# A two-branch encoder layer: the first request group's head by channel quarters, branch B's inverse rms through DRAM, the gate's adaLN in column strips

## The chip, the cores and the metric

The kernel runs on one core of a Trainium2 chip. The metric is the device time of one execution in microseconds (us), taken as the median of several runs. TensorE, VectorE, ScalarE and GpSimd compute, each with its own stream of instructions; all DMAs are issued from SyncE's queue.

## What is computed

The same layer, with the same weights, is applied to two request groups (prompt and sample), each 1024 tokens of 1024 channels, all in float32.

```python
mod = silu(c) @ w_ada + b_ada
shift, scale, gate = split(mod, 3)
h = rms_norm(x, norm_g) * (1 + scale) + shift
qa, ka, va, za, qb, kb, vb, zb, ga, gb = split(h @ w_in)
# branch A: 8 query heads, 2 key/value heads of 64; QK rms norm, axial rotary
oa = attention(qa, ka, va) * silu(za)
# branch B: 4 heads, two softmax maps each, values of 128
ob = softmax(q1 k1) v - lam * softmax(q2 k2) v
ob = rms_norm(ob, subln_g) * (1 - lam_init) * silu(zb)
merged = sigmoid(ga) * (oa @ w_proj_a) + sigmoid(gb) * (ob @ w_proj_b)
y = x + gate * (merged @ w_out)
```

## The kernel before

Every large product is made in three matmuls: each operand is held as a rounded high part and a low part (`split_w`, L175: ScalarE rounds, VectorE subtracts), and high x high, high x low and low x high are added up in PSUM. `x` is held with channels on the partitions: eight chunks of 128 channels, two halves of 512 tokens (`ht[hf]`, the normalised rows, as high and low parts). One bank of a gate product (`z_gen`, L693: za, zb, ga, gb) is 24 matmuls of 512 columns at L704; there are 48 banks in each group, in 12 items of four. One tile of 128 tokens of a q, k or v product (`proj_tt`, L506) is 24 matmuls of 256 columns at L515.

**The head of the first group** (`start`, L337). adaLN's shift and scale are made from eight loads of 1 MB of `w_ada` (`load_ada`, L243), each with four float32 matmuls of 512 columns whose stationary operand is `cT`, two columns (`ada`, L292, L298). `ada_end` (L300) copies the two rows, turns them into columns with four small matmuls (L307) and adds the bias (L311, L315). The first 512 tokens' squares (L254) are added up on VectorE (`added`, L257) and summed over the partitions by matmuls with a column of ones (`inv_rms`, L266, L271); GpSimd takes the power, `spread` (L281) makes of it a tile over all partitions. `modulated` (L317) scales, shifts and splits. The second 512 tokens' squares aren't added first, so L271 runs eight times as often for them; `start_late` (L368) modulates them. Projections come behind all adaLN matmuls. The key/value weights are loaded early into `p` tiles; the other weights pass through three `st` tiles.

**Order.** The kernel writes its pieces of work as generators, and `weave` (L71) sets their order: of several streams, each with a nominal number of steps and an offset, the one with the least progress is next. A scheduler then orders each engine's instructions with that order as priority, by a model of time, and can pull later work forward where buffers allow. `head` (L1020) weaves the key/value products (`kva_gen`), the first half of branch A's queries (`qa_gen`) and gate banks (`Z_HEAD`, in banks). Then `phase` (L1115) weaves six stages of attention: two of branch A's 16 units and four of branch B's four, each with the next products and with `Z_SHARE` gate banks. In the last stage `fill` (L1142) runs beside the attention: for the first group the gate's adaLN (`gate_gen`, L445; 16 loads, 16 float32 matmuls at L452), the gate banks that are left, and the first `16 - TAIL` merge pieces of branch A (`merge_gen`, L954; 12 matmuls of 512 columns at L976 each). `TAIL` merge pieces stand behind the attention, then branch B's merge, then the output product (L1007) with the second group's normalisation beside it.

**An attention unit** has scores (L737, L738), a maximum on VectorE (L739), the exponential on ScalarE (L741), for branch B a difference of two maps (L773), a block transpose on VectorE (L774) with four DMAs that put the blocks in place (`flip`, L767, L779), and the values (L799, L800 or L839). Branch B's squares are summed by matmuls at L861; GpSimd takes the inverse rms (L869) once a head's four units are through.

**Gating** (`gated_gen`, L912) reads attention output and gate back from DRAM, multiplies them with the row factor, and splits. Branch A's row factors (inverse softmax sums) are transposed once, written to a DRAM row `rA` (L921), and read back spread over the partitions into `tab` tiles (L936; two buffers, which also hold the rotary tables). Branch B's are transposed by TensorE into a PSUM bank, four transposes for each half of each head (L942); VectorE multiplies from there (L943, L947).

Tiles come from pools: 15 `u` tiles of 1 MB, two `w` tiles for split weights, four `p`, three `st` and three `row` tiles, one `ev` tile; in PSUM two `s` tiles of two banks (scores), three `f` banks and one `a` bank. `gbank` (L120) also hands out score banks while no attention runs.

## Time and profile before

| | |
|---|---|
| median of 3 runs | 1940.68 us (1940.3 to 1945.74) |
| the profiled execution | 1933.24 us |
| its span, first to last instruction | 1931.5 us |
| mean granted TensorE clock | 0.995 |
| first exponential of the first group's attention | 141.5 us |
| last matmul at L452 (gate's adaLN) | 767.8 us |
| last power of branch B's inverse rms, first group | 849.4 us |

The lines below are from the profiled execution. A row of the timeline gives start, duration, engine, line, operation and tiles (`f<-u,cT` is: writes `f`, reads `u` and `cT`), the count of instructions merged in it, and in brackets how long the engine stood idle before it and what it waited for. A row of the chain of waits gives start, duration, and the engine, tile and line on the chain. A row of a group gives busy time, mean duration in ns, idle time before. A row by stretches gives the stretch, its length, busy time with number of instructions on each engine (TensorE, its weight loads, VectorE, ScalarE, GpSimd), the granted clock, the DMA engines' share and GB/s. A float32 matmul shows as two rows.

### The profile page before, as it was taken

To read this page: it belongs to the slowest core of one execution; us is meant where nothing else is said; L and a number is where in the kernel's file an instruction comes from. 1 tells how busy PE (TensorE), PEld (TensorE's weight loads), DVE (VectorE), ACT (ScalarE), POOL (GpSimd) and SP (SyncE) were. 2 spreads that over 40 slices of the span, in tenths; PEclk is the share of its full clock that TensorE was granted. 3 is DMA by queue.
4 is the path that set the end of the run, shared out by engine and by line. 5 is a ranking of instruction groups with operands and counts; after the bars stand their busy time and mean duration, and the time that the engine had idled before them with its cause. 6 is when DMAs were issued, how large, how long until landed. Compare 5 with 4: busy or idle time off the path is not lost.

```text
span 1931.5 us, 30797 instructions
## 1 busy us (share of the span) xinstructions
PE 1881.2 (97%) x10466; PEld 1610.0 (83%) x10466; DVE 1397.3 (72%) x2145; ACT 991.7 (51%) x2091; POOL 414.7 (21%) x758
## 2 busy tenths in 40 slices
PE   8899999999999999999999999999989999999999
PEld 3788888888988995778889888898877989888887
DVE  5669886778898677767465788688788767777731
ACT  4446665666666454414233566566666545542310
POOL 1342300120335051000124231013221524201000
PEclk9999999999999999999999999999999999999999
DMA  9125465556554436875641455565545343477522
GB/s 319 45 81 146 135 173 148 153 148 176 152 142 110 116 92 192 273 256 181 218 140 39 137 144 166 145 172 151 154 129 162 107 113 100 143 234 264 180 104 77
DMA packets 271613, 295.25 MB, mean 153 GB/s; under 512 B 37857, under 2 KB 220257, under 8 KB 271457
## 3 DMA queue, kind: packets, MB, share of 16 engines
q1 hardware_dynamic: 271456, 293.28, 51.4%
q8 instruction: 84, 1.38, 0.3%
q14 instruction: 73, 0.59, 0.1%
HBM read 133.72 MB, written 42.01 MB: 91 GB/s over the span
## 4 chain that ended last, share of the span: by engine, by line
PE 81%; DVE 7%; DMA 5%; issue 2%; ACT 2%; SPq 1%; POOL 1%; DVEq 0%; ACTq 0%; POOLq 0%
PE f L704 22%; PE f L515 19%; PE f L1007 5%; PE s L737 5%; PE a L839 5%; PE s L738 5%; PE f L976 4%; PE s L1007 4%; PE a L800 3%; PE a L799 3%; PE s L976 2%; DMA q<-p 2%; DVE m L739 2%; DVE p L774 1%; PE f L298 1%
## 5 line engine op out<-in xcount | busy, mean ns | idle before, releaser
L704 PE MATMUL f<-u,w 128*128 128x512 f32 x2232 | 574.2, 395 | 2.0 <-DVE ssB L863 1.5
L515 PE MATMUL f<-w,u 128*128 128x256 f32 x3456 | 487.5, 285 | 7.5 <-DVE u L571 3.7
L515 PEld LDWEIGHTS f<-w,u 128*128 128x128 f32 x3456 | 457.8, 190 | 29.0 <-DVE u L571 4.3
L704 PEld LDWEIGHTS f<-u,w 128*128 128x128 f32 x2232 | 404.2, 188 | 77.8 <-DVE ssB L863 1.8
L739 DVE TENSOR_REDUCE m<-s 128x1 f32<-128x1024 f32 x256 | 311.0, 1217 | 51.3 <-PE s L738 48.4
L774 DVE STREAM_TRANSPOSE p<-p 128x1024 f32<-128x1024 f32 x192 | 238.3, 1241 | 92.7 <-ACT p L741 89.3
L738 PE MATMUL s<-u,sw 128*128 128x512 f32 x512 | 203.8, 398 | 0.0
L788 DVE TENSOR_TENSOR q<-q,hi 128x512 fp32r<-128x512 f32 x256 | 171.5, 690 | 34.3 <-ACT hi L787 32.3
L787 ACT ACTIVATE hi<-q 128x512 fp32r<-128x512 f32 x256 | 153.6, 624 | 76.2 <-DMA q<-p 37.8
L741 ACT ACTIVATE p<-s,m,rsA 128x1024 f32<-128x1024 f32 x128 | 153.8, 1202 | 71.4 <-DMA q<-p 69.6
L178 ACT ACTIVATE w<-st 128x512 fp32r<-128x512 f32 x196 | 114.4, 625 | 99.2 <-DMA st<-in_w_in_dram 42.4
L741 ACT ACTIVATE p<-s,m,rsB 128x1024 f32<-128x1024 f32 x128 | 154.3, 1205 | 6.5 <-DMA q<-p 1.9
L179 DVE TENSOR_TENSOR w<-st,w 128x512 fp32r<-128x512 f32 x196 | 132.8, 706 | 34.2 <-ACT w L178 33.1
L658 POOL TENSOR_TENSOR row<-row,gB 128x96 f32<-128x96 f32 x64 | 33.8, 528 | 485.7 <-ACT row L529 474.1
L799 PE MATMUL a<-hi,u 128*128 128x256 f32 x512 | 132.2, 284 | 2.8 <-DMA q<-p 1.8
L800 PE MATMUL a<-q,u 128*128 128x256 f32 x512 | 129.3, 286 | 2.6 <-DVE q L788 2.6
L976 PE MATMUL f<-u,w 128*128 128x512 f32 x540 | 130.5, 393 | 1.3 <-DVE u L987 1.3
L839 PE MATMUL a<-q,u 128*128 128x256 f32 x512 | 127.1, 385 | 3.9 <-DVE oo L816 3.0
L976 PEld LDWEIGHTS f<-u,w 128*128 128x128 f32 x540 | 100.5, 188 | 23.0 <-DVE u L987 2.3
L839 PEld LDWEIGHTS a<-q,u 128*128 128x128 f32 x512 | 95.6, 193 | 20.0 <-DVE oo L816 3.6
L737 PE MATMUL s<-u 128*128 128x512 f32 x256 | 108.3, 424 | 3.3 <-ACT p L741 3.2
L737 PE MATMUL s<-u,u 128*128 128x512 f32 x256 | 102.4, 400 | 8.5 <-ACT p L741 3.1
(181 smaller groups left out, 2557.5 us busy)
## 6 DMA issues: line engine op xcount, KB each, us to landing
q<-p SPq DMA_DIRECT2D x768, 128.0 KB, 2.6
st<-in_w_in_dram SPq DMA_DIRECT2D x132, 256.0 KB, 3.1
zd<-ev SPq DMA_DIRECT2D x96, 256.0 KB, 2.2
sw<-u SPq DMA_DIRECT2D x256, 64.0 KB, 2.1
p<-zd SPq DMA_DIRECT2D x64, 256.0 KB, 3.7
u<-in_w_ada_dram SPq DMA_DIRECT2D x8, 1024.0 KB, 10.4
st<-in_w_in_dram SPq DMA_DIRECT2D x64, 128.0 KB, 2.8
st<-in_w_out_dram SPq DMA_DIRECT2D x32, 256.0 KB, 3.6
```

The lines of the kernel that those rows point to most:

```text
L515: nc.tensor.matmul(ps, lt[c][:, sl], w[:, c, wi, :], start=(k == 0), stop=(k == 23))
L704: nc.tensor.matmul(ps, w[:, c, wi, e * P : (e + 1) * P], rt[c], start=(k == 0), stop=(k == 23),)
L737: nc.tensor.matmul(s[:, sl], q, k[:, sl], start=True, stop=False)
L738: nc.tensor.matmul(s[:, sl], sw, k[:, sl], start=False, stop=True)
L739: nc.vector.tensor_reduce(out=m, in_=s, axis=AX.X, op=ALU.max, negate=True)
L741: nc.scalar.activation(pt.rearrange("p (j c a) -> p j c a", j=4, c=8), s.rearrange("p (c a j) -> p j c a", c=8, j=4), AF.Exp, scale=rs, bi ...
L774: nc.vector.transpose(pt, pt)
L799: nc.tensor.matmul(acc, lt, th[:, c, :], start=(k == 0), stop=False)
L800: nc.tensor.matmul(acc, lt, tl[:, c, :], start=False, stop=(k == 7))
L839: nc.tensor.matmul(acc, u["v"][:, k], pT[:, k], start=(k == 0), stop=(k == 7))
L976: nc.tensor.matmul(ps, w[:, c, wi, d * P : (d + 1) * P], o[:, oi, :], start=(k == 0), stop=(k == 11))
L1007: nc.tensor.matmul(ps, w[:, c, wi, e * P : (e + 1) * P], m[:, mi, :], start=(k == 0), stop=(k == 23))
```

## The change

- **The first group's head goes by channel quarters.** `xT` is loaded first; an adaLN load now holds shift and scale of 256 channels, so two loads give a quarter. Its matmuls go to four column strips of the array (`tile_position`), one for each input chunk, with `cT` padded to 32 columns; the strips' sums are added by four small matmuls with a two-column selector (`ada_sum`). For each quarter: multiply by the inverse rms, modulate, the key/value and za products of its two channel chunks (`kva_early`, `z_one`, into four and two PSUM regions held open), then the next quarter's adaLN. za's first weights are loaded early too, za's second go into `u` tiles. These instructions keep their program order on their engines (`in_order`).
- **The late rows** (second 512 tokens): squares added up on VectorE first; their inverse rms and modulation are split into two calls; modulated in two halves. za's four banks for them are made chunk by chunk (`z_first`).
- **The gate's adaLN** moves to the head, woven with `qa`, in loads of 256 by 256 and matmuls of 256 columns in four column strips.
- **Branch B's inverse rms**: 16 rows (two heads) are transposed at once, copied, written to DRAM (`rB`) and read back spread into a `tab` tile, as branch A's.
- **Numbers**: shares, weights and offsets of `weave`, now per group where they weren't.

```diff
-    (7, 19, 6, 3, 2, 4),
-    (9, 14, 7, 3, 2, 6),
+    (8, 23, 6, 1, 1, 2),
+    (13, 12, 7, 3, 0, 6),
 )
-Z_HEAD = (6, 5)
+Z_HEAD = (9, 6)
...
-LAST_ATT = 44
-LAST_FILL = 26
-GATED_A = -0.3
-TAIL = 5
-TAIL_A = 0.3
+LAST_ATT = (45, 45)
+LAST_FILL = (20, 25)
+GATED_A = (0.12, 0.1)
+GATE_A = 0.0
+TAIL = (2, 3)
+TAIL_A = (1.15, 1.15)
+Z_FIRST = (22, 7)
+Z_FIRST_A = (-0.05, -0.1)
...
+        total, *rest = [q[:, i : i + 2] for q in sq for i in (0, 2)]
+        for x in rest:
+            nc.vector.tensor_tensor(out=total, in0=total, in1=x, op=ALU.add)
+        nc.vector.tensor_tensor(out=total[:, 0], in0=total[:, 0], in1=total[:, 1], op=ALU.add)
...
+    def ada(wts, cpad):
+
+        acc = gbank()
+        for q, wt in enumerate(wts):
+            for c in range(4):
+                pe.matmul(
+                    acc[32 * c : 32 * c + 32], cpad[:, q * 4 + c], wt[:, c], start=(q == 0), stop=(q == 1),
+                    tile_position=(0, 32 * c),
+                )
+        part = rtile()
+        act.activation(part, acc, AF.Copy)
+        return part
...
     def modulated(ht, hf, xT, cs):
         for c in cs:
             scale, shift = modc[:, 1, c, 0:1], modc[:, 0, c, 0:1]
+            hh, hl = (x[c] for x in ht[hf][:2])
+            act.activation(hh, xT[c], AF.Identity, scale=scale, bias=shift)
+            vec.tensor_scalar(
+                out=xT[c], in0=xT[c], scalar1=scale, scalar2=shift, op0=ALU.mult, op1=ALU.add
+            )
+            vec.tensor_tensor(out=hl, in0=xT[c], in1=hh.bitcast(F32), op=ALU.subtract)
...
+        rs = inv_rms(added(squares(xT[0])))
+        rsb = spread(rs)
+        early.update(kva=[x for b in two_banks() for x in (b[:, :256], b[:, 256:])], z=two_banks())
+        ps = ada_sum(ada(wts[:2], cpad))
+        for quarter in range(4):
+            cs = range(quarter * 2, quarter * 2 + 2)
+            by_rms(xT[0], cs, rsb)
+            split_early(kva_w[0][1], quarter)
+            ada_end(quarter, ps)
+            if quarter % 2 == 0:
+                add_h(ht, 0, quarter // 2)
+            split_early(kva_w[1][1], quarter, act)
+            modulated(ht, 0, xT[0], cs)
+            split_early(kva_w[1][1], quarter, vec)
+            for c in cs:
+                kva_early(ht, c)
+            part = ada(wts[quarter * 2 + 2 : quarter * 2 + 4], cpad) if quarter < 3 else None
+            for c in cs:
+                for e in range(2):
+                    z_one(ht, 0, c, kva_w[1][0], e, early["z"][e], pe)
+                if part is not None:
+                    ps, part = ada_sum(part), None
+        xT.append(load_xT0(1))
+        kva_w.append((load_w(w_cols(w_in, (C_ZA + 256, 256)), room=(utile(), utile())),))
+        return lambda: inv_rms(added(squares(xT[1]))), lambda rs: start_late(ht, xT[1], rs)
...
+                for c in (2, 3, 0, 1):
+                    nc.tensor.matmul(
+                        acc[32 * c : 32 * c + 2], cT[:, q * 4 + c], sts[c // 2][:, c % 2], start=(q == 0), stop=(q == 1),
+                        tile_position=(0, 32 * c),
+                    )
...
+        banks = [two_banks(), two_banks()]
+        for c in range(NCH):
+            for w, bs in zip(ws, banks):
+                for e, ps in enumerate(bs):
+                    z_one(ht, 1, c, w, e, ps)
+            yield 1
...
+        if i > 1 and hf == 0:
+            ss = st["ssB"][:, 2 * i - 4 : 2 * i - 2].rearrange("p j n -> p (j n)")
+            ps = fbank()[:16, :P]
+            nc.tensor.transpose(ps, ss, ident)
+            row = rtile()[:16, :P]
+            nc.scalar.activation(row, ps, AF.Copy)
+            dma(st["rB"][i - 2], row)
...
-                rb = gbank()
-                for k in range(4):
-                    r = st["ssB"][:, e - 4, hf * 4 + k : hf * 4 + k + 1]
-                    nc.tensor.transpose(rb[:, k * P : (k + 1) * P], r.to_broadcast([P, P]), ident)
+                dma(rb, rB[e % 2, hf].partition_broadcast(P))
...
-            for i in range(2):
-                weave((islice(kva, 6), 6, 0.0), (islice(zs, 3), 3, 0.0))
-                if i == 0:
-                    late()
-            weave((chain(kva, qa), 40, 0.0), (islice(zs, nz - 6), nz - 6, Z_HEAD_A[g]))
+            rs = late[0]()
+            drain(islice(zs, 6))
+            late[1](rs)
+            weave((kva, 27, 0.0), (islice(zs, Z_FIRST[0]), Z_FIRST[0], Z_FIRST_A[0]))
+            weave((qa, 27, 0.0), (islice(zs, Z_FIRST[1]), Z_FIRST[1], Z_FIRST_A[1]), (gate_gen(), 8, GATE_A))
...
         def fill():
-            if g == 0:
-                yield from gate_gen()
             yield from zs
             drain(first)
-            yield from islice(merge, 16 - TAIL)
+            yield from islice(merge, 16 - TAIL[g])
```

303 lines of the change are left out of this document (170 added, 133 removed).

## Prediction

> **What bounds the kernel now.** I read the page first (shares, slices, chain of waits), then windows by stage, then groups and timeline of the head.
>
> ```profile
> span 1931.5 us, 30797 instructions
> PE 1881.2 (97%) x10466; PEld 1610.0 (83%) x10466; DVE 1397.3 (72%) x2145; ACT 991.7 (51%) x2091; POOL 414.7 (21%) x758
> PE 81%; DVE 7%; DMA 5%; issue 2%; ACT 2%; SPq 1%; POOL 1%; DVEq 0%; ACTq 0%; POOLq 0%
> ```
>
> TensorE is busy for 97% of the span and holds 81% of the chain. So matmuls that vanish are worth their issue time, unless their stage falls to another engine. Stages, with columns PE, PEld, DVE, ACT, POOL, granted clock, DMA share, GB/s: head of the first request group, its last three attention stages (two rows), and the second group's stages around 1450.
>
> ```profile
> 0.00:142.00 142.00, 124.87 (x702) 92.31 (x703) 85.38 (x211) 62.54 (x147) 41.86 (x68) 0.98 0.45 151
> 581.00:738.00 157.00, 157.00 (x967) 140.21 (x966) 115.64 (x173) 83.58 (x190) 61.26 (x125) 1.00 0.40 110
> 738.00:850.00 112.00, 105.93 (x451) 76.41 (x451) 81.30 (x117) 43.95 (x85) 6.47 (x14) 1.00 0.79 257
> 1260.00:1450.00 190.00, 180.53 (x1091) 159.76 (x1090) 154.11 (x220) 125.53 (x268) 48.97 (x99) 0.98 0.56 152
> 1450.00:1519.00 69.00, 65.06 (x344) 55.69 (x343) 54.40 (x79) 40.31 (x86) 16.05 (x35) 0.95 0.52 143
> ```
>
> TensorE idles 17 us in the head and 6, 9 and 4 us in the other rows that aren't full; between 581 and 738 it never does. What the head's busy time consists of, by groups up to 142 us, and how fast a row of each kind issues, by the chain:
>
> ```profile
> L515 PE MATMUL f<-w,u 128*128 128x256 f32 x384 | 50.6, 285 | 3.3 <-DVE ev L712 3.1
> L704 PE MATMUL f<-u,w 128*128 128x512 f32 x78 | 19.8, 396 | 0.0
> L704 PE MATMUL s<-u,w 128*128 128x512 f32 x48 | 14.0, 437 | 0.0
> L271 PE MATMUL f<-ones_c,q 128*128 128x1 f32 x72 | 10.2, 271 | 0.0
> 29.68 10.39 PE f L298 x24
> 45.35 7.18 PE f L271 x50
> 112.12 3.65 PE f L704 x16
> 115.78 2.88 PE f L515 x24
> ```
>
> One row costs 0.43 us at L298 (adaLN), 0.144 at L271, 0.228 at L704 and 0.12 at L515. Useful work (projections) by 142 us is 384 x 0.12 + 126 x 0.228 = 75 us, with some 4 us of transposes and first scores. The other 63 us are adaLN (64 rows, 28 us), row sums (10), the wait for the first load, and gaps.
>
> **The change, part by part.** *1. The first quarter.* Channel quarters let projections start after 4 MB of loads (xT, then the first two adaLN pieces), where now all adaLN work goes first:
>
> ```profile
> 6.85 9.21 PE L298 MATMUL f<-u,cT 128*2 128x512 f32 x16 [6.85 <-DMA u<-in_w_ada_dram]
> 13.36 2.40 ACT L254 ACTIVATE q<-u 128x512 f32<-128x512 f32 x4 [0.22 <-DMA u<-in_xT_prompt_dram]
> 14.54 1.23 DVE L260 TENSOR_TENSOR q<-q,q 128x1024 f32<-128x1024 f32 x1 [4.90 <-ACT q L254]
> 29.38 0.60 ACT L287 ACTIVATE ev<-s 128x512 f32<-128x512 f32 x1 [3.71 <-PE s L285]
> 29.92 0.17 DVE L315 TENSOR_TENSOR modc<-modc,gcol 128x8 f32<-128x8 f32 x1
> 31.87 0.81 ACT L321 ACTIVATE u<-u,modc 128x512 f32<-128x512 f32 x1 [1.89 <-POOL u L356]
> 41.88 1.70 PE L515 MATMUL f<-w,u 128*128 128x256 f32 x12
> 44.47 2.50 DVE L327 TENSOR_TENSOR u<-u,u 128x512 fp32r<-128x512 f32 x4 [1.07 <-ACT u L326]
> ```
>
> The same 4 MB (in another order) are in by 14 us, when the last squares start. The squares, their sum and the inverse rms fit beside the load of the adaLN pieces, xT being first. Then the quarter's 16 adaLN rows: 5 us, as TensorE starts cold (0.58 us a row in the first fence line here). Then the partial sums' copy (0.6, as L287's), their sum (0.6, four small matmuls, an estimate), modc (two steps of 0.17), ScalarE's 0.81 and the low part's 0.63: 3 us. First projection at 22 us, against 41.88.
>
> *2. The pitch of a quarter.* Useful: 24 x 0.12 + 12 x 0.228 = 5.6 us. The next quarter's 16 adaLN rows go in four column strips. No row shows strips: at the one end they don't overlap, 6.9 us; at the other all four do, 1.7. A float32 matmul is two instructions (64 rows for 32 matmuls) which both write one strip, so in order each can pair with its neighbour's half only: I take 3.4. The modulation behind it is covered by one channel of L704 rows (1.4 us) and leaves 1.2. Pitch 10.2, so four quarters end at 22 + 3 x 10.2 + 5.6 = 58 us with 22.4 us done: 36 not useful, 31 with full overlap, 46 with none.
>
> ```profile
> 13.32 0.09 PEld L298 LDWEIGHTS f<-u,cT 128*2 128x2 f32 x1 [0.34 <-issue]
> ```
>
> The Trainium skill, "TensorE: Matmul & The Clock Gate", Part 3, has matmuls in different column strips start about 4 ns apart, 2.38 times for three strips; by it the rows would cost 1.7 to 2.2 us a quarter, and the sum would be some 5 us lower. The same section says that a weight load overlaps a running matmul only where the row groups differ, which strips of all rows never do; by that, no gain. The row above speaks against this: loads of one row group start every 0.43 us while a matmul runs. "TensorEngine Tiling (Array Packing)", Key Properties, adds that a change of the tiling mode drains the engine, which no run here shows; it would add a few us.
>
> *3. The late rows.* Their squares now add up on VectorE (three sums of 1.23 as L260's and one of half the size: 4.4 us) and cost 8 rows for 64 at L271: -8 us of TensorE, and no stretch at half clock:
>
> ```profile
> 49.00:56.00 7.00, 7.00 (x26) 6.28 (x27) 2.56 (x14) 0.72 (x2) 1.21 (x2) 0.52 0.44 144
> ```
>
> VectorE has some 5.4 us of work in a 10 us quarter (eight passes over 512 elements at 0.6 or so, as L327's, and modc), so the sums hide; then the two remaining gate banks of the early rows (48 x 0.228 = 11 us) cover the late modulation. If that cover falls short, up to 10 us; I take 4. Of the row chains' gaps up to 142 us (some 12) I keep 6. Head: 36 + 4 + 6 = 46 us not useful against 63: **-17** (-32 to +5).
>
> *4. The gate's adaLN* moves from the last attention stage into the head and goes in strips:
>
> ```profile
> L452 PE MATMUL f<-st,cT 128*2 128x512 f32 x32 | 15.2, 592 | 1.2 <-DMA st<-in_w_ada_dram 1.2
> L942 PE MATMUL f<-ident,ssB 128*128 128x128 f32 x60 | 8.9, 273 | 0.8 <-DVE u L987 0.8
> 852.25 0.60 PE L942 MATMUL f<-ident,ssB 128*128 128x128 f32 x4
> 58.00:142.00 84.00, 74.58 (x501) 67.86 (x500) 57.12 (x150) 39.14 (x106) 35.30 (x56) 1.00 0.19 58
> ```
>
> 32 x 0.429 = **-13.7** there, **+6.9** in the head (3.4 to 13.7). Its 16 loads go past the flips on SP's queue; in the head's later part the DMA engines are busy for 0.19 (last row), so they wait for nobody there.
>
> *5. Branch B's rms by a DRAM row*: 64 transposes at 0.11 us leave, **-7**, and the four new ones add 0.4. In their place come a write and broadcast reads, like those of branch A today (KB each, us to landing):
>
> ```profile
> tab<-rA SPq DMA_DIRECT2D x32, 128.0 KB, 3.8
> rA<-row SPq DMA_DIRECT2D x2, 32.0 KB, 2.3
> 849.36 1.97 POOL L869 TENSOR_TENSOR ssB<-ssB,nhalf 128x8 f32<-128x8 f32 x1
> 854.00 0.68 DVE L947 TENSOR_TENSOR row<-f,row 128x512 f32<-128x512 f32 x1
> ```
>
> Today VectorE multiplies 2.7 us after the power ends at 851.3. Copy, write and read make that 6.5, or more where the read waits on SP with the flips behind it. Today five merge pieces of 12 x 0.228 = 2.7 us stand after the last attention step; TAIL leaves two or three. Nothing below (the other merges cover it) to 10 us for each group; I take **+4** in all.
>
> *6. Pieces set anew.* The first group's head takes 11.7 gate banks for 6, and the shares then use up all 48 by its first B stage; today they last to 850:
>
> ```profile
> 581.00:738.00 157.00, 28.79 (x111) 20.29 (x111) 1.00 0.40 110
> 738.00:850.00 112.00, 32.04 (x120) 22.33 (x120) 1.00 0.79 257
> 142.00:318.00 176.00, 85.68 (x332) 59.01 (x330) 1.00 0.54 147
> 134.00:260.00 126.00, 119.72 (x692) 104.13 (x691) 111.61 (x155) 83.36 (x176) 32.69 (x44) 1.00 0.54 149
> ```
>
> The first three are L704's rows alone. 231 x 0.228 = 53 us of filler leave 581 to 850. It isn't lost, since earlier stages keep TensorE full, but 269 - 53 - 14 - 3 = 199 us of TensorE's work then stand beside 115.6 + 81.3 = 197 of VectorE's. VectorE was never above 89% in a long stretch (last row), so 197 / 0.89 = 221: a loss of 22 us, if nothing is pulled forward. The third row shows that pieces are pulled forward: 13.8 banks ran in a stage whose share is 7. I take **+8** (0 to 53). The second group's shares and weights touch 13 idle us in the two stages around 1450; without a row for the new order I take **-4** (-13 to +10).
>
> Sum: -17 - 13.7 + 6.9 - 6.6 + 4 + 8 - 4 = **-22 us**. The profiled execution took 1933.24 us, 1.7 around its span, and becomes 1911. The median of the runs shown is 7.4 above it (1940.68), so a median of **1919**.
>
> **The rivals.** *Strips all beside each other*: -5 in the head and -3.4 at the gate: 1910. For it: nothing in the old trace orders strips. Against: the two halves of one matmul. The skill's Part 3 is this case. *Strips don't overlap*: 46 for 36 in the head, 13.7 for 6.9 at the gate, +17: 1936. For it: every row at L298 issues 0.43 us behind the one before, whatever it writes. *The last attention stages of the first group starve TensorE* (slower): they stay as long as today but for the gate and the transposes, since each unit's scores, reduction, flip and values follow one another; then all 53 us of moved filler are paid again: -22 + 45 = 1964. It decides from a loss of 30 us in 581 to 850 on, where the rest of the sum is used up. For it: VectorE's 197 us; against: TensorE had 263 busy us of 269 there, so latency alone didn't set the pace. That quarters don't start early after all (the queue delivering adaLN before xT) would cost the 17 us of the head, and lies inside the range.
>
> **How the numbers follow.** A measurement of this kernel tells some 0.3% (6 us) from no change. Forecast 0.52, full overlap 0.2, no overlap 0.15, starved stages 0.13. Faster: 0.49 + 0.2 + 0.06 = 0.75; same: 0.02 + 0.09 = 0.11; slower: 0.01 + 0.13 = 0.14. The range takes in the head's better end (-15), a pull-forward without loss (-8) and the second group's (-9), and on the other side no overlap with a loss of 16 in the starved stages: 1887 to 1945; beyond it lie the starved case and a few more in a hundred.
>
> **What would show it.** Right: L515's rows from about 22 us on; quarters 10 us apart; adaLN rows issuing at 0.2 us or so; no half clock near 50 us; no transposes between merges, with VectorE's multiply some 6 us behind the power. Wrong: first projections after 30 us, quarters over 13 us apart, TensorE below 90% between the second B stage and the merges, or stalls before the second branch's first merge piece of over 5 us. The prediction fails above all if the filler moved to the head is missed later.

## The result and the profile after

The changed kernel takes 1955.02 us (median of 4 runs, 1954.29 to 1957.15) where the kernel before takes 1941.57 beside it: 1.0067 times as long, with an interval of 1.005 to 1.0085. The forecast was 1919 (1887 to 1945), so the sign is wrong. The profiled span grew by 21.1 us (1931.5 to 1952.6), more than the medians, because the profile of before lies 8 us below its own median and that of after does not. What follows compares profiles, so its terms add up to 21 and not to 13.

The page of the changed kernel: span, busy time of the engines, granted clock in 40 slices, chain of waits.

```profile
span 1952.6 us, 30738 instructions
PE 1866.7 (96%) x10406; PEld 1607.9 (82%) x10406; DVE 1399.9 (72%) x2174; ACT 986.1 (50%) x2087; POOL 400.9 (21%) x756
PEclk9999999999999998899999999999999999999999
PE 65%; DVE 13%; DMA 9%; SPq 4%; ACT 4%; issue 3%; POOL 2%; DVEq 0%; ACTq 0%; POOLq 0%
```

TensorE has less to do, but its share of the chain falls from 81% to 65%; VectorE and the DMAs take it over. Two slices are granted some 0.8 of the clock: they lie in the third and the fourth (last) of the first group's four B stages. By stretches of the changed kernel: the head, then the last three attention stages, then the tail of the merges.

```profile
0.00:180.00 180.00, 153.12 (x927) 124.02 (x928) 105.06 (x259) 67.53 (x152) 37.59 (x66) 0.96 0.51 158
638.00:720.00 82.00, 78.32 (x537) 72.42 (x536) 61.00 (x89) 45.33 (x101) 30.13 (x67) 1.00 0.42 105
720.00:779.00 59.00, 52.35 (x283) 44.07 (x282) 52.00 (x82) 37.72 (x86) 26.74 (x58) 0.88 0.47 124
779.00:870.00 91.00, 75.66 (x307) 58.66 (x307) 69.96 (x97) 32.92 (x66) 6.89 (x12) 0.91 0.71 200
870.00:1110.00 240.00, 235.26 (x1225) 201.19 (x1224) 144.13 (x284) 79.22 (x177) 49.85 (x71) 0.99 0.50 162
```

The same last stage and tail before:

```profile
738.00:811.00 73.00, 68.51 (x279) 46.03 (x279) 54.49 (x74) 34.18 (x67) 4.21 (x9) 1.00 0.76 236
811.00:1078.00 267.00, 265.42 (x1385) 227.10 (x1384) 169.78 (x324) 87.71 (x190) 49.64 (x71) 1.00 0.52 173
```

The second and third stage together shrank from 157 us (581 to 738 before) to 141, but the last one grew from 73 to 91, at a clock of 0.91 for 1.00. Idle time is the better measure. I count for each matmul the time at which it can issue behind the one before at full clock (0.227 us for 512 columns, 0.12 for 256, and so on, as in the prediction) and call the rest of a stretch lost; time at half clock counts as lost for its half. By that count TensorE's work fell by 41 us (1843 to 1802) and the time lost rose by 61 (89 to 150). Of the 61, 39 arise between the first B stage and the second group's first exponential (16 us lost there before, 55 after); most of the rest, some 16, arise before the first exponential (25 us lost there before, 41 after).

What is missing in those stages shows in the rows of the gate products (L817) alone, in the last three attention stages of the changed kernel:

```profile
638.00:720.00 82.00, 0.00 (x0) 0.00 (x0) 1.00 0.42 105
720.00:779.00 59.00, 0.00 (x0) 0.00 (x0) 0.88 0.47 124
779.00:870.00 91.00, 0.00 (x0) 0.00 (x0) 0.91 0.71 200
```

Before, 231 such rows stood there (111 and 120 in the prediction's lines). In their place the last stage now has 168 rows of merges (L1088), where it had none before; so its length alone isn't comparable, and the merges behind it are shorter for it.

A second view of the same: the lag, which is the time at which W us of the matmuls that every version has in common (1785 us in all; adaLN, row sums and the transposes of the inverse rms are left out) have been issued, less W. In us:

| W | before | after | head alone (e6) | gate strips alone (h2) |
|---|---|---|---|---|
| 50 | 60 | 45 | 46 | 61 |
| 100 | 64 | 50 | 46 | 65 |
| 150 | 66 | 62 | 52 | 67 |
| 200 | 69 | 64 | 52 | 71 |
| 450 | 73 | 70 | 56 | 76 |
| 650 (before the last attention stage) | 76 | 82 | 82 | 80 |
| 700 (within it) | 99 | 114 | 119 | 108 |
| 750 | 103 | 121 | 160 | 116 |
| 1250 | 112 | 135 | 173 | 135 |
| end | 143 | 164 | 220 | 172 |

The head does gain: 15 us at W = 50. Of that, 11 are gone by 150, where the tables and the gate come in. From 450 to 750 the changed kernel loses 51 us where the old one loses 30, and 14 of the 30 were the gate's rows, which the changed kernel no longer has there. The second group runs at nearly the old lag.

### The profile page after: what moved, and what is told of

Same layout as the page of the kernel before. It is cut to its first block, busy times and chain, and to the rows that moved or that the text cites. A ratio compares the mean times of both kernels' runs of the same rounds, so it can differ in the third digit from the quotient of the medians.

```text
span 1952.6 us, 30738 instructions
## 1 busy us (share of the span) xinstructions
PE 1866.7 (96%) x10406; PEld 1607.9 (82%) x10406; DVE 1399.9 (72%) x2174; ACT 986.1 (50%) x2087; POOL 400.9 (21%) x756
## 4 chain that ended last, share of the span: by engine, by line
PE 65%; DVE 13%; DMA 9%; SPq 4%; ACT 4%; issue 3%; POOL 2%; DVEq 0%; ACTq 0%; POOLq 0%
PE f L593 16%; PE f L817 15%; PE f L1119 6%; PE f L1088 4%; PE s L844 4%; PE s L845 4%; DMA q<-p 4%; PE a L946 3%; PE s L1119 3%; DVE m L846 3%; SPq L886 3%; PE a L907 2%; PE a L906 2%; DVE p L881 2%; DMA row<-zd 2%
## 5 line engine op out<-in xcount | busy, mean ns | idle before, releaser
L817 PE MATMUL f<-u,w 128*128 128x512 f32 x1992 | 510.1, 394 | 4.7 <-ACT ev L774 3.2
L593 PE MATMUL f<-w,u 128*128 128x256 f32 x3360 | 466.6, 285 | 1.2 <-ACT ev L774 1.1
L593 PEld LDWEIGHTS f<-w,u 128*128 128x128 f32 x3360 | 440.3, 191 | 20.6 <-issue 2.2
L817 PEld LDWEIGHTS f<-u,w 128*128 128x128 f32 x1992 | 361.5, 189 | 74.1 <-ACT ev L774 4.5
L197 ACT ACTIVATE w<-st 128x512 fp32r<-128x512 f32 x188 | 109.3, 625 | 90.6 <-DMA st<-in_w_in_dram 35.0
L1088 PE MATMUL f<-u,w 128*128 128x512 f32 x588 | 147.6, 403 | 5.7 <-DVE u L1061 3.4
L198 DVE TENSOR_TENSOR w<-st,w 128x512 fp32r<-128x512 f32 x188 | 127.1, 705 | 29.5 <-ACT w L197 28.8
L1088 PEld LDWEIGHTS f<-u,w 128*128 128x128 f32 x588 | 112.5, 194 | 33.5 <-DVE u L1061 5.7
L737 POOL TENSOR_TENSOR row<-row,gB 128x96 f32<-128x96 f32 x64 | 29.3, 457 | 474.1 <-ACT row L607 459.0
L845 PEld LDWEIGHTS s<-u,sw 128*128 128x128 f32 x512 | 98.7, 193 | 15.9
```

The source lines that it names most:

```text
L593: nc.tensor.matmul(ps, lt[c][:, sl], w[c][:, wi, :], start=(k == 0), stop=(k == 23))
L817: nc.tensor.matmul(ps, w[c][:, wi, e * P : (e + 1) * P], rt[c], start=(k == 0), stop=(k == 23),)
L845: nc.tensor.matmul(s[:, sl], sw, k[:, sl], start=False, stop=True)
L1088: nc.tensor.matmul(ps, w[:, c, wi, d * P : (d + 1) * P], o[:, oi, :], start=(k == 0), stop=(k == 11))
```

## The experiments

The theories by their letters in the expectations: **S**, the last attention stages of the first group are starved, because the filler (gate banks, the gate's rows) went to the head; **T**, SyncE issues the tables of branch B late and the head pays; **R**, the DRAM row stalls the second branch's merge; **C**, any new order costs some per cent by chance of the scheduler; **P**, merge pieces in the last stage take the `p` tiles of the attention; **N**, the stage numbers fit only the structure that they were made for.

**Is it chance?** `c1_control` is the kernel before with one nominal count changed, `h1_rows_added` adds up the late rows' squares first, which is one part of the head.

```diff
-LAST_ATT = 44
+LAST_ATT = 45
```

> The kernel before with one number of the last stages' order changed by a step (LAST_ATT 45 for 44); no work is added or taken. Theory S says nothing of it: within 5 us, 1936 to 1947. Rival C: 1950 to 1970.

It took 1943.22 us, 1.0013 times before (0.9996 to 1.0029). So C is out for this one step in the kernel before. The changed kernel got no such control, and five edits of it below (e2, e3, m1, t1, t2) came out 5 to 22 us slower than it; there C stays open. The control also shows how far two profiles differ without a cause: by the count above its profile loses some 12 us more than that of before, and it has 42 us at half clock for 20.

```diff
-        rs = inv_rms([q[:, c] for q in squares(xT[1]) for c in range(4)])
+        rs = inv_rms(added(squares(xT[1])))
```

> The kernel before with the late rows' squares added up on VectorE ahead of the sums over partitions, one part of the change alone: 56 rows of 0.112 to 0.144 us leave TensorE, and the half clock near 50 us with them. If TensorE's work in the head counts in full: 1930 to 1935 us. If the order set by the scheduler decides (rival C): 1945 to 1965.

It took 1943.73 us, 1.0014 (1.0 to 1.0029): no gain. Head of this kernel, in the view by stretches (0 to 142 us stands in the prediction for before):

```profile
0.00:143.00 143.00, 121.16 (x643) 87.97 (x644) 88.81 (x215) 62.25 (x147) 41.92 (x68) 0.94 0.45 150
```

The 56 small rows are gone (702 to 643 rows in about the same stretch), but the first exponential comes no sooner (142.8 us for 141.5, and 143.9 in the control): what TensorE no longer does is lost in pauses. The granted clock of 0.94 for 0.98 isn't the edit's doing, since the control's unchanged head has 17 us at half clock too. In h1 it starts at 45.0 us behind a pause of 5.2 us, in which TensorE waits for weights that ScalarE rounds; the kernel before has its small rows there.

**The numbers and the structure.** `e5_numbers_alone` gives the kernel before the new shares, weights and offsets; `e1_numbers_back` gives the changed kernel the old ones.

```diff
-    (7, 19, 6, 3, 2, 4),
-    (9, 14, 7, 3, 2, 6),
+    (8, 23, 6, 1, 1, 2),
+    (13, 12, 7, 3, 0, 6),
...
-LAST_ATT = 44
-LAST_FILL = 26
+LAST_ATT = (45, 45)
+LAST_FILL = (20, 25)
...
```

> The kernel before with the stage numbers of the changed one, nothing else of the change. Theory S: filler runs out in the old structure also, but six banks and the gate's 13.7 us later, so 1940 to 1955 us, with idle TensorE in the last stages of the first group. Rival R: the numbers are harmless, 1935 to 1943.

> The changed kernel with the stage numbers of before (shares, weights, offsets of the six stages, TAIL 5, fill 26); the new head, the gate's place and the DRAM row stay. Theory S (the filler for TensorE is spent too early, so that the last attention stages of the first group starve it; the changed kernel's 50 us windows from 750 to 900 us hold 46 us without a matmul, before 10): most of it comes back, 1925 to 1940 us. Rival R (the DRAM row for branch B's rms delays the merges and blocks the flips): 1948 to 1955. Rival N (the second group's stages got worse): its last two stages (15 + 5 us idle) get 10 us shorter, the first group's stay.

The first took 1995.75 us, 1.0272 (1.0255 to 1.0289), the second 2006.34, 1.0328 (1.031 to 1.0346). Each set of numbers loses some 50 us in the other's structure, more than any answer on record. So the new numbers are a repair and not the damage: they are the price at which the new head is borne.

**Parts undone.** `e3_gate_back` puts the gate's rows, still in strips, back into the last stage; `e2_row_back` puts the transposes back for the DRAM row.

```diff
-            weave((qa, 27, 0.0), (islice(zs, Z_FIRST[1]), Z_FIRST[1], Z_FIRST_A[1]), (gate_gen(), 8, GATE_A))
+            weave((qa, 27, 0.0), (islice(zs, Z_FIRST[1]), Z_FIRST[1], Z_FIRST_A[1]))
...
+            if g == 0:
+                yield from gate_gen()
```

> The changed kernel with the gate's adaLN back in the last attention stage, still in column strips. Theory S: some 4 us of filler and 4 MB of loads return there and leave the head, so little changes: 1948 to 1958 us. If moving the gate itself cost the time (it was 13.7 us of filler), the strips would be the reason, and the time stays too; under a rival by which the gate's loads stall the head (a 4.4 us gap ahead of its last sum at 171 us), 1945 to 1950.

It took 1976.06 us, 1.0175 (1.0157 to 1.0193), slower than every answer. The head is 9 us shorter at W = 200, but the last stage:

```profile
787.00:888.00 101.00, 78.02 (x337) 57.60 (x338) 75.06 (x115) 37.40 (x73) 5.23 (x9) 0.83 0.81 239
```

101 us for 91, at a clock of 0.83. The gate's rows in strips, back in this stage, don't fill it.

```diff
-                dma(rb, rB[e % 2, hf].partition_broadcast(P))
+                rb = gbank()
+                for k in range(4):
+                    r = st["ssB"][:, e - 4, hf * 4 + k : hf * 4 + k + 1]
+                    nc.tensor.transpose(rb[:, k * P : (k + 1) * P], r.to_broadcast([P, P]), ident)
...
```

> The changed kernel with branch B's inverse rms by TensorE's transposes into a PSUM bank again, nothing else. Theory S: 7 us of TensorE work return into stages that have idle time, 1950 to 1958 us. Rival R: 1935 to 1945, and the waits ahead of the first merge of branch B are gone.

It took 1977.38 us, 1.0181 (1.0165 to 1.0196): 22 us slower than the changed kernel, which neither answer had. In the profile some 7 of them are the transposes, 10 more are lost in the merges behind the attention and 7 in the second group. R as the cause of the whole loss is out.

**Parts alone.** `e4_row_alone` is the kernel before with the DRAM row and nothing else.

```diff
-                rb = gbank()
-                for k in range(4):
-                    r = st["ssB"][:, e - 4, hf * 4 + k : hf * 4 + k + 1]
-                    nc.tensor.transpose(rb[:, k * P : (k + 1) * P], r.to_broadcast([P, P]), ident)
+                dma(rb, rB[e % 2, hf].partition_broadcast(P))
...
```

> The kernel before with branch B's inverse rms by the DRAM row, nothing else of the change. By the prediction's sum: 7 us of transposes go and some 4 us of waits come, 1935 to 1941. Rival R (the detour through DRAM stalls the first merges of branch B): 1945 to 1955.

It took 1948.37 us, 1.003 (1.002 to 1.0041): 6 us slower. Its merges and output product, by stretches:

```profile
818.00:1088.00 270.00, 262.54 (x1353) 223.35 (x1352) 168.77 (x322) 87.37 (x192) 49.50 (x71) 1.00 0.53 178
```

It has 32 matmul rows fewer than the old tail, yet is 3 us longer: 3.5 us of transposes went, and 7 us of lost time came.

`h2_gate_strips` is the kernel before with the gate's adaLN in strips, in its old place.

```diff
-            acc = gbank()[:2]
-            for k in range(NCH):
...
-                dma(st, w_ada[k * P : (k + 1) * P, col : col + 512])
-                nc.tensor.matmul(acc, cT[:, k], st, start=(k == 0), stop=(k == NCH - 1))
...
+            acc = gbank()[:, :256]
+            nc.vector.memset(acc, 0.0)
...
+                for c in (2, 3, 0, 1):
+                    nc.tensor.matmul(
+                        acc[32 * c : 32 * c + 2], cT[:, q * 4 + c], sts[c // 2][:, c % 2], start=(q == 0), stop=(q == 1),
+                        tile_position=(0, 32 * c),
+                    )
...
```

> The kernel before with one edit: the gate's adaLN stays in the last attention stage but goes in sets of four column strips, 8 sets of 0.61 us where 32 rows of 0.43 us stand. Theory: TensorE's work in the last stages sets the pace of the kernel before, so 13.7 - 4.9 = some 9 us go, 1932 (ratio 0.995), and TensorE's idle time in that stage stays near 8 us. Rival: the stage is held by its chain of scores, reduction, flip and values, and the gate's rows only fill it, so the time stays within 5 us of 1941 and the idle time of that stage grows by about what the rows lose.

It took 1965.11 us, 1.0121 (1.0106 to 1.0136). Neither answer had it: with 9 us of TensorE's work less the kernel is 23 us **slower**. By stretches, its last stage and its tail:

```profile
742.00:822.00 80.00, 71.70 (x327) 54.01 (x326) 56.83 (x84) 34.24 (x67) 6.21 (x9) 0.89 0.77 228
822.00:1097.00 275.00, 267.78 (x1381) 228.82 (x1379) 167.78 (x323) 86.89 (x191) 51.57 (x71) 0.99 0.51 165
```

The stage is 7 us longer than the old one, at 0.89 for 1.00, and the tail 8. (The profiles differ by 30 us; the other 15 lie before the stage and in the second group, where the edit changes nothing.) Ten microseconds from the part with the gate's rows, first in h2:

```profile
750.00:760.00 10.00, 7.53 (x36) 4.06 (x36) 9.47 (x14) 5.46 (x12) 0.68 (x2) 0.83 0.72 203
```

then in the kernel before:

```profile
748.00:758.00 10.00, 8.88 (x30) 3.56 (x29) 8.10 (x12) 6.16 (x12) 0.69 (x2) 1.00 0.74 234
```

With the long rows TensorE is busy for 8.9 of 10 us and the clock is full; with the strips it is busy for 7.5, though part of that is at half speed. Closer, in stretches of 3.4 us (within 0.3 us of those in which the clock changes), h2:

```profile
749.50:752.90 3.40, 1.36 (x9) 0.75 (x5) 3.40 (x5) 2.14 (x5) 0.00 (x0) 0.96 0.44 119
752.90:756.30 3.40, 3.40 (x14) 1.66 (x15) 2.92 (x4) 1.59 (x3) 0.34 (x1) 0.54 0.88 254
773.40:776.80 3.40, 1.65 (x12) 0.78 (x12) 2.73 (x4) 1.75 (x6) 0.34 (x1) 0.96 0.84 197
776.80:780.20 3.40, 3.40 (x15) 2.64 (x10) 2.22 (x3) 1.47 (x3) 0.00 (x0) 0.50 0.71 257
```

and the kernel before, at its longest pause of that stage (2.0 us, ending at 793.9), which falls on the border of two such stretches:

```profile
789.70:793.10 3.40, 2.23 (x10) 1.50 (x8) 3.21 (x5) 1.37 (x3) 0.00 (x0) 1.00 0.84 283
793.10:796.50 3.40, 2.60 (x11) 2.17 (x12) 3.29 (x6) 3.37 (x8) 0.00 (x0) 1.00 0.81 246
```

Where TensorE was busy for 1.36 or 1.65 of 3.4 us, the next 3.4 us were granted half the clock; where it kept 2.2 and 2.6, the clock stayed. Slow matmuls then lengthen the scores for which VectorE and ScalarE wait, and that, I take it, opens the next pause. The clock goes with the time over all runs of this pair: 0.981 to 0.986 in the four of h2, 0.990 to 0.994 in the seven of the kernel before beside them. In the last stage h2 has 17 us at half clock, where the profiles of before, control, h1 and e4, which keep the long rows, have 0, 7, 0 and 0. But the edit also gives VectorE four tiles to clear, and VectorE stands 3.9 us for the gate's sums in this stage (1.2 before); no run separates the two.

`e6_head_alone` is the other half of the same question: the new head, with stage numbers, branch B's transposes and the gate's place as before (the gate's rows in strips).

```diff
-    (8, 23, 6, 1, 1, 2),
-    (13, 12, 7, 3, 0, 6),
+    (7, 19, 6, 3, 2, 4),
+    (9, 14, 7, 3, 2, 6),
...
-            weave((qa, 27, 0.0), (islice(zs, Z_FIRST[1]), Z_FIRST[1], Z_FIRST_A[1]), (gate_gen(), 8, GATE_A))
+            weave((qa, 27, 0.0), (islice(zs, Z_FIRST[1]), Z_FIRST[1], Z_FIRST_A[1]))
...
```

> The changed kernel with only its head: the stage numbers, the gate's rows (in strips) in the last attention stage and branch B's transposes as in the kernel before. Theory that the head's gain is real by itself and lost by what is done with its filler: the numbers of before were set for a head without 31 us of gate pieces, so shares run out sooner, the last stage idles 20 us or more, and the time is 1960 to 2000. Rival, that numbers set for another structure cost little where the last stage keeps its own gate rows: 10 to 18 us faster than before, 1923 to 1931.

It took 2011.55 us, 1.0363 (1.0345 to 1.038), slower than S said. The table of lags shows both halves: 52 for 69 at W = 200, a full 17 us gained, and 160 for 103 at W = 750. The last stage:

```profile
774.00:889.00 115.00, 85.35 (x362) 63.04 (x360) 77.41 (x118) 39.52 (x75) 4.64 (x9) 0.78 0.69 203
```

115 us for 73, at 0.78. The head's gain is real; the gate banks that it used up are missed.

**Filler given back.** `d1_after_filled` adds 216 small matmuls, whose results aren't used, to the last three attention stages of the changed kernel (432 rows of 0.109 us, 47 us); `d2_before_filled` adds the same to the kernel before.

```diff
+        def idle_work():
+            for _ in range(6):
+                ps = fbank()
+                for k in range(12):
+                    nc.tensor.matmul(ps[:, (k % 4) * P : (k % 4 + 1) * P], ident, ident, start=True, stop=True)
+                    if k % 6 == 5:
+                        yield 1
...
+                phase(2 + h, *fs, more=((idle_work(), 12, 0.0),) if g == 0 and h else ())
...
```

> The changed kernel with 216 float32 matmuls of 128 columns added that compute nothing that is used (some 0.22 us each, 47 us in all), a third of them as a third stream beside each of the last three attention stages of the first group. Theory S (those stages starve TensorE): the added work falls into idle time, so the time rises by 5 to 25 us, to 1960 to 1980, and the half clock between 750 and 900 us goes. Rival (the stages are bound by TensorE, and the time is lost elsewhere): plus 40 to 50, 1995 to 2005. Rival C (any other order of the schedule costs some 20 us by itself, as four edits have now done): this run and the one beside it rise alike.

> The kernel before with the same 47 us of unused matmuls in the same three stages. Theory S: there TensorE is full, so the time rises by 40 to 55 us, to 1982 to 1998. Rival C: it rises as far as the changed kernel does.

They took 1989.78 us, 1.0254 (1.0227 to 1.0281), and 1992.59, 1.0259 (1.0237 to 1.0281): some 36 us more for the changed kernel, between S and its rival, and 50 more for the old one, as S said. So some 14 us (each of the two is known to about 5) of free TensorE time took up work at no cost, in the second and third stage, where lost time fell from 19 us to 4 and half clock from 13 us to none. The last stage was no better for it:

```profile
796.00:898.00 102.00, 84.28 (x391) 68.92 (x389) 70.47 (x95) 33.45 (x66) 4.26 (x9) 0.88 0.65 188
```

27 us are still lost there. Filler helps where it is ready when TensorE pauses; here it isn't.

`s1_banks_kept` keeps gate banks back from the earlier stages; by the trace seven of them then stand in the last three attention stages, where the changed kernel has none.

```diff
-    (8, 23, 6, 1, 1, 2),
+    (8, 17, 4, 1, 1, 2),
...
-LAST_FILL = (20, 25)
+LAST_FILL = (23, 25)
```

> The changed kernel with some five gate banks of the first group moved from its second A stage and first B stage into the last stage (shares 17 and 4 for 23 and 6), LAST_FILL 23 for 20. Theory S (merge pieces, which wait for gated operands, are all the filler that is left in the last stage): idle time of TensorE there falls from 24 to some 10 us, and the A stage loses up to 8; 1940 to 1952. Rival (the last stage is bound by the attention's own chain, whatever stands beside it): 1955 to 1965.

It took 1945.97 us, 1.0024 (1.001 to 1.0038): 8 to 9 us better than the changed kernel, the best version of it, and as S said. The second A stage, where most of the banks were taken, and the last stage:

```profile
364.00:555.00 191.00, 176.66 (x1026) 154.50 (x1025) 151.39 (x217) 122.97 (x259) 45.61 (x93) 0.96 0.58 148
773.00:845.00 72.00, 65.09 (x273) 53.37 (x273) 58.40 (x80) 35.55 (x68) 5.97 (x9) 0.92 0.77 231
```

The last stage is back at 72 us, and the last three B stages lose 19 us for 44; but the A stage now loses 28 for 9. Filler is short as a whole: some 31 us more of it than before stand in the head, and each bank can be spent once. `s2_head_kept` takes the seven gate pieces from the second part of the head instead (`Z_FIRST = (22, 0)`, shares 8, 21, 4).

> The changed kernel with 2.3 gate banks less in the head (none beside the first queries), shares 21 and 4 for 23 and 6, so that five to six banks are left for the last stage, LAST_FILL 23. Theory S as the run with five banks kept left it (it gained 9 us, of which the A stage lost 19): the head's last stretch loses some 5 us and the A stage less than there: 1940 to 1950. Rival (filler is short in all stages alike, so its place doesn't matter): 1950 to 1960.

It took 1947.21 us, 1.0041 (1.0025 to 1.0057): the same as s1 within the intervals.

**The last stage.** `m1_merge_unbound` lets the first group's branch A merges of that stage read tiles that are ready, and `p1_no_gate_tile` has them load no gate and so take no `p` tile. What they leave out: in m1 branch A's part of the first output isn't made from its gated rows; in p1 branch A's gate is missing from the first output.

```diff
+                        if st is states[0] and not br:
+                            o = st["qkb"][3][0][:, :, hf * 512 : hf * 512 + 512]
```

> The changed kernel whose first group's branch A merges read a tile that is ready long before (query rows of branch B) in place of the gated output; the gating is still computed, and its result isn't used by those merges, so branch A's part of the first output is left out. Theory S, in the form that the merges wait for the gating: they fill the last stage from its start, and 12 to 20 us go, 1935 to 1943. Rival (the attention's chain sets the last stage): within 5 us of 1955.

It took 1960.49 us, 1.0093 (1.0077 to 1.0108), and its last stage loses 24 us as in the changed kernel, so the merges' wait for their rows isn't what holds the stage.

```diff
-                    if d % 2 == 0:
+                    if st is states[0] and not br:
+                        pass
+                    elif d % 2 == 0:
...
```

> The changed kernel whose first group's branch A merges take no p tile and load no gate (they read a tile that is there already, so the gate of branch A is left out of the first output). Theory P (merge pieces are the only filler left in the last stage, and their gate tiles take the four p tiles from the attention: 16 such loads between its first and last exponential, before 2; ScalarE waits 16.7 us for p tiles there, before 0): TensorE's idle time in the last stage falls from 24 us to under 14, and 10 to 20 us go, 1935 to 1945. Rival (the attention's own chain, with its flips, sets the stage): within 5 us of 1955.

It took 1949.58 us, 1.0058 (1.0034 to 1.0081). For P, by tile `p` in the last stage: the gate loads, and what ScalarE waited for such tiles, in the changed kernel:

```profile
L1079 SPq DMA_DIRECT2D p<-zd x16: 320/426/587, 795.8 to 868.5; - x16
  ACT p L848: 16.7, 8
```

before:

```profile
L967 SPq DMA_DIRECT2D p<-zd x2: 430/450/470, 800.7 to 801.7; - x2
```

and the last stage of p1, by stretches:

```profile
779.00:849.00 70.00, 57.60 (x224) 44.66 (x223) 62.10 (x84) 31.80 (x63) 8.04 (x12) 0.88 0.67 190
```

In the changed kernel the stage's filler is merge pieces, 16 gate loads for 2, and they compete with the exponentials for four tiles. Without these loads ScalarE's waits for `p` tiles fall to 2.4 us and the stage takes 70 us for 91. But some 18 of these 21 us are TensorE work that is only made later (five merge pieces, 14 us, above all), and 21 us are still lost where P said under 14. The whole is 2 to 5 us better, within the intervals (1.0058 for 1.0067). So the waits for `p` tiles are real, but the runs don't show that they cost the time.

**The tables.** `t1_tables_free` takes the tables' DMAs out of the fixed program order; `t2_tables_sooner` loads the tables right behind the late rows' modulation.

```diff
-                dma_next(dst[:, a], t[src].rearrange("(n p) d -> p n d", p=P))
+                dma(dst[:, a], t[src].rearrange("(n p) d -> p n d", p=P))
...
```

> The changed kernel with the loads of branch B's tables (cosB, sinB, gains, lambda) no longer held in program order on SyncE's queue; nothing else. Theory T (VectorE stands at the tables' steps for 6.5 and 2.3 us near 160 to 170 us, since those loads now start at 157 us instead of 39, and TensorE stops 4.4 us and runs 6.8 us at half clock for it): 8 to 12 us come back, 1943 to 1947. Rival (that stretch has other work to wait for): within 3 us of 1955.

```diff
+            load_tables_B()
...
-        if g == 0:
-            load_tables_B()
```

> The changed kernel with branch B's tables loaded and scaled right behind the late rows' modulation, in program order, instead of behind the head. Theory T (VectorE's wait for these loads near 160 us stops TensorE and halves its clock): 6 to 10 us go, 1945 to 1949, and the lag behind the projections' work stays near 52 us up to the first scores (62 now). Rival (any place costs as much, as the run with the loads let free showed: 10 us lost near 55 us): 1953 to 1960.

They took 1972.73 us, 1.0147 (1.0118 to 1.0176), and 1961.9, 1.0113 (1.0092 to 1.0134), both slower than any answer. The stall that they aim at is real. The timeline of the changed kernel:

```profile
165.59 0.20 DVE L484 TENSOR_SCALAR gB<-gB 128x64 f32<-128x64 f32 x1 [6.49 <-DMA gB<-in_qn_b_dram]
169.75 0.37 DVE L495 TENSOR_TENSOR p<-p 128x128 f32<-128x128 f32 x1 [2.25 <-DMA p<-in_lam_k_dram]
171.08 0.77 PE L534 MATMUL s<-two,row 128*128 128x2 f32 x4 [4.10 <-DVE row L531]
```

VectorE stands 6.5 and 2.3 us for the tables, with the rest of its queue behind them; the gate's sum (L534) waits 4.1 us behind it on TensorE, and 6.8 us of half clock follow. But tables loaded sooner cost 9 or 10 us at W = 50 (a lag of 54 to 56 for 45). So T names a place where time goes, and no place was found where the tables are free. `b1_kept_sooner` puts t2 and s1 together:

> The changed kernel with five banks kept for the last stage and the tables right behind the late rows. If both causes are apart, their gains add up: 1946 less 6 to 10, 1936 to 1940, no slower than the kernel before. If the order of the rest decides: 1946 to 1960.

It took 1956.72 us, 1.0082 (1.0057 to 1.0107): the two don't add. No version of the changed kernel beats the kernel before.

## Why the prediction was wrong, step by step

**Steps 1 and 2, the quarters: right.** The timeline of the changed kernel's head and gate:

```profile
23.88 0.50 PE L99 MATMUL s<-w,u 128*128 128x256 f32 x2 [1.31 <-ACT u L99]
29.25 1.92 PE L99 MATMUL f<-u,at 128*32 128x512 f32 x16
38.97 1.92 PE L99 MATMUL f<-u,at 128*32 128x512 f32 x16
162.55 0.61 PE L525 MATMUL s<-st,cT 128*2 128x256 f32 x8
```

The first projection starts at 23.9 us (22 was forecast), a quarter takes 9.7 us (10.2), and a quarter's adaLN 1.9 us: the end of full overlap (1.7), not the 3.4 that I took. So that rival's premise held, but its 5 us don't show: the start is 2 us later than forecast, each pitch is only 0.5 us shorter, since the four sums take 0.8 us of it that the working left out, and the fourth quarter's products come at 58.9 us, behind the late rows' sums.

**Step 3, the late rows: right in the sum, wrong in the reason.** The head alone (e6) gains the 17 us forecast at W = 200. That it is exactly 17 is luck: the strips did better than the sum had it, while the 8 us for the row sums aren't on the path (`h1_rows_added`), and half clock did not go. Profiles of the old head have 7 us of it (before) to 17 (the control), those of the new one 7 (e6) to 20 (m1).

**Step 4, the gate.** In the head it costs 9 us (lag of after against e3 at W = 200: 64 for 55), where 6.9 was forecast; 4.9 of that are its eight sets of 0.61 us, the rest its place behind the tables. The -13.7 in the last stage fails: `h2_gate_strips` takes 9 of them away in place and is 23 us slower, some 15 of them in that stage and its tail. Those rows weren't only load on TensorE; they filled its waits, and it seems that they kept its clock up too. They don't do so in every order: with the new numbers (e5) the last stage has 14 us at half clock although it has the long rows.

**Step 5, the row: right in its delay, wrong in the sum.** The power, from the chain of waits, then the write, the read and the multiply, from the timeline of the changed kernel:

```profile
885.94 1.66 POOL ssB L976
888.25 0.32 SPq L1035 DMA_DIRECT2D rB<-row  x1
890.27 0.80 SPq L1054 DMA_DIRECT2D tab<-rB  x2
894.17 0.68 DVE L1059 TENSOR_TENSOR q<-tab,q 128x512 f32<-128x512 f32 x1
```

From the power's end (887.6) to the multiply are 6.6 us; 6.5 was forecast. But alone the row costs 6 us, where -2.6 was forecast (-6.6 and +4).

**Step 6, the pieces: the step that failed.** "I take +8 (0 to 53)" for the first group; the lost time of its four B stages and its merges rose from 16 to 55 us, so +39. This is the rival of starved stages, which got 0.13 and 1964; it named 30 us as the point where it decides, and 1955 came. The working had two errors.

First, it let the stages be paced by VectorE at 0.89: 221 us. That fits the third stage (52.0 busy of 59), but in the last one VectorE is busy for 70 of 91 us and no engine is full. What is left to set that one is steps that wait for one another (scores, reduction, flip, values, and the merges' own); this is argued, and no run shows which. "TensorE had 263 busy us of 269 there, so latency alone didn't set the pace" was the false argument: it was busy because filler had been put into each wait, and TensorE's work could leave without the waits leaving. Filler put back shows it (d1 in the second and third stage, s1 in all three). The forecast's own sign of being wrong came too: TensorE is busy for 88.7% of the third stage and 83% of the last, under the 90% that it named.

Second, the working priced an idle TensorE at its idle time only. Half clock rose from 20 to 58 us over the span by the clock's record, and at half speed 38 us more of it cost 19 of the 61 lost. The profile of before, at a clock of 0.995, is among the best of its kind: 60 runs of that kernel beside the experiments have 0.989 to 0.996, with a median of 0.991, and the four of the changed kernel 0.983 to 0.985. From these I estimate 35 us and 62 at half clock in typical runs, so 27 more and some 14 us lost by it.

The second group's -4 (-13 to +10) came out at about 0: 38 us lost in it before and after.

**What stays open.** Why p1's last stage still loses 21 us though its `p` tiles are free, and why d1's filler isn't taken up there. That half clock feeds the pauses that bring it is argued from the stretches of 3.4 us and from h2; no run could hold the clock fixed. Why the numbers of one structure cost 50 us in the other is seen only in its result. S foresaw the four runs that add filler or move it (d1 in part), but the edits that undo or add a part (e1, e2, e3, e5, e6) cost more than any answer on record; how much of that is the new order as such isn't separated.

## What to carry to other kernels

Before work is taken from an engine that is busy for 97%, ask of each stage whether the engine is busy because it is the bound or because waits were filled; compare the stage's length with its chain of dependent steps. Filler is a stock: what a faster head uses up early must be replaced in the stages whose waits it hid. Where a stage has waits, look at TensorE's busy time in each 3.4 us too: in h2 9 us of work less came with more half clock and 23 us more in all.

## What the runs showed of the hardware

- **Half clock follows a half-idle window.** In the records of four kernels (before, after, h2, e6) every half-clock stretch of one run begins at the same phase of a period of 3.41 us and lasts a multiple of it. Of full-clock periods with under 1.5 us of busy TensorE all 29 were followed by half clock; of those over 1.8, all but four were not (two with 1.95 and 2.16, and two of the old head, in before and h2, that the profile shows as full of the one-column rows at L271); between them both occur. Back to full speed it needs more: every period at half clock with under 2.8 busy us was followed by another, and so were some fuller ones. The phase differs from run to run (from the span's start 1.04 us in before, 0.71 in after, 1.71 in h2, 1.35 in e6), so the same pause may fall into one period or be split over two; that this makes the clock of one kernel vary (0.989 to 0.996 in 60 runs of before) is not shown. The Trainium skill, "TensorE: Matmul & The Clock Gate", Part 1, has the same window of 3.4 us but speaks of a whole idle window ahead of the slow clock; the measured rows above, 1.36 and 1.65 us busy of 3.4, go before it.
- **Four column strips of float32 cost about as much as one.** 16 adaLN rows of 512 columns take 1.92 us, where the old head issues one row every 0.43 us (6.9 for 16). The Trainium skill, the same page, Part 3, has 4 ns between starts of packed matmuls; the records here have 6 to 7 within a set of four, and sets 0.43 us apart. The Trainium skill's sentence there that a weight load overlaps a running matmul only in other row groups isn't borne out. The weight loads beside the second fence line of the quarters:

```profile
29.24 0.16 PEld L99 LDWEIGHTS f<-u,at 128*32 128x32 f32 x8
29.70 0.13 PEld L99 LDWEIGHTS f<-u,at 128*32 128x32 f32 x4 [0.30 <-issue]
30.13 0.13 PEld L99 LDWEIGHTS f<-u,at 128*32 128x32 f32 x4 [0.30 <-issue]
```

  These use all rows of the array, and stand within the 1.92 us of the matmuls.
